# Where the operands of TensorE start in memory: a transformer kernel with longer tiles and shifted activations

## The chip, the core and the metric

The kernel runs on one core of a Trainium2 chip. The metric is the device time of one execution in microseconds (us), the median of several runs; lower is better.

## The reference, cut to what matters

Two blocks follow each other on 256 tokens of width 1024, in fp32. The first block runs two layers, the second one. Every layer is a projection of the normed input, a mixer (attention, a gated recurrence or a convolution), an output projection and a feed-forward network (FFN):

```python
for l in range(DEPTH):                       # 2 layers
    h = rmsnorm(x, norm_mix[l])
    proj = h @ w_in[l]
    ...
    merged = jax.nn.sigmoid(ga) * (y_attn @ w_proj_attn[l]) + jax.nn.sigmoid(gb) * (y_hgrn @ w_proj_hgrn[l])
    x = x + merged @ w_out[l]
    h = rmsnorm(x, norm_ffn[l])
    g, u = jnp.split(h @ w_ffn_in[l], 2, axis=-1)
    x = x + (jax.nn.silu(g) * u) @ w_ffn_out[l]
```

The second block does `[attn, u] @ w_o` and one more FFN, with its inputs scaled and shifted by a vector from `c @ ada_w`.

## The kernel before

All large products run on TensorE in the type fp32r, each as three matmuls: an operand is split into a high part H and a rest L, and H·H, H·L and L·H are summed (`mm3`, L781). ScalarE makes H with a copy, VectorE makes L with a subtraction (`split_into`, L887; `do_split`, L720, for the weights). In every matmul one operand is stationary (loaded by its own instruction, 128 columns) and the other is moving (streamed past it).

- **Moving activations, stationary weights.** In `pair_mm` (L786), `proj_mm` (L795) and `out_mm` (L896) the weights `wH`, `wL` are stationary, 128 columns at a time, and 256 tokens of an activation move: `xH`, `xL` (the normed input, `act_pair`, L873), `ya` and `yh` (the mixer's outputs, tiles `b4`, L1162 and L1289), `mH`, `mL` (the merged output, tiles `E`, L1314) and `H`, `L` of the FFN (tiles `t512`, L1382). The profile calls these moving tiles x, b, E and t.
- **Stationary activations, moving weights.** In `token_mm` (L804), `first_tm` (L1332) and `out_tm` (L908) the activations are stationary and 512 columns of weights move. `out_tm` is the second block's output projection and its FFN's.

In `out_mm` and `pair_mm` matmuls of the FFN interleave: the output product of one step of 256 hidden units runs beside the input product of the next (`ffn`, L1355). Nothing of this order is written by hand: the kernel records its operations (`Recorder`, L350), and a list scheduler with its own costs, due times and buffer counts (`issue`, L428) gives every engine its order. The costs of fp32r matmuls there follow from the number of columns alone.

Weights come through a ring of 4 raw tiles and 6 pairs `wH`, `wL` (`weights`, L734), all DMAs from SyncE's queue.

A tile has an address per partition. The tiles lie one after the other in the order of their first use, after a region of 16384 bytes that is kept for dynamic DMAs. All lengths are rounded up to 128 bytes (`new`, L644). A constant `GAP` (L755) of 256 bytes pads the constants, and `PLACE = 28` words puts `xH` and `xL` 112 bytes into tiles that are 128 words longer than they need be. The layout that comes out, as the start of the operand modulo 256 bytes:

| operand | base of its tile | start |
|---|---|---|
| weights raw, wH, wL | 0 | 0 |
| xH, xL | 0 | 112 |
| b4 (ya, yh) | 0 | 0 |
| E (mH, mL) | 128 | 128 |
| t512 (H, L of the FFNs) | 128 | 128 |

E and t512 lie at 128 because the tile `em` (L1010), a single line of 128 bytes, comes ahead of them. Within a tile, slices of an fp32r operand follow each other at multiples of 512 bytes. Every one of these starts is the same modulo 512 too.

Of the kernel before, what the change touches and what calls it, by code (L numbers as in the profile page):

```python
# [15 lines left out]
F32 = mybir.dt.float32  # L16
F32R = mybir.dt.float32r
# [10 lines left out]
FF, NJ = 2816, 11  # L28
LINE = 128

GAP = 64

PLACE = 28
OUT_SHAPE = [256, 1024]
EPS = 1e-6
NEG = -1e30
# [583 lines left out]
def program(tc, I, out, pw, cw, tap=None, stop=None):  # L620
    nc = tc.nc
# [10 lines left out]
    with es:  # L632
# [3 lines left out]
        act = es.enter_context(tc.tile_pool(name="act", bufs=1))  # L636
        tmp = es.enter_context(tc.tile_pool(name="tmp", bufs=2))
# [3 lines left out]
        def body():  # L641
            uid = [0]

            def new(pool, shape, dt=F32, tag=None, bufs=None):  # L644
                n = int(np.prod(shape[1:]))
                line = LINE if dt == U8 else LINE // 4
                if pool is not psum and pool is not dram and n % line:

                    v = new(pool, [shape[0], -(-n // line) * line], dt, tag, bufs)[:, :n]
                    return v if len(shape) == 2 else v.rearrange("p (a b) -> p a b", a=shape[1])  # L650
                uid[0] += 1
                b = Buf(pool, shape, dt, f"{tag or 'c'}_{uid[0]}", tag, bufs or 1, "PSUM" if pool is psum else "SBUF")
                return View(b, np.arange(n).reshape([1] + list(shape[1:])), shape[0], ())

            def bank(tag="mm"):
                return new(psum, [128, 512], F32, tag=tag, bufs=4)

            def acc_banks():

                acc = [bank("side") for _ in range(4)]  # L660
                for a in acc[1:]:
                    a.buf.group = acc[0].buf.group
                return acc

            def t512(dt=F32):
                return new(tmp, [128, 512], dt, tag="t512", bufs=9)

            def b4(dt=F32):
                return new(act, [128, 1024], dt, tag="b4", bufs=11)

            def small(n, bufs=8):
                return new(tmp, [128, 32], F32, tag="small", bufs=bufs)[:, :n]
# [1 line left out]
            def v2(ap):  # L674
                return ap.rearrange("p (a b) -> p a b", a=2)

            def bc(ap, n):
                return ap[:, None, :].to_broadcast([ap.shape[0], n, ap.shape[1]])
# [18 lines left out]
            def P(name):  # L697
                o, n = pw[name]
                return prm[:, o:o + n]
# [32 lines left out]
            at = [0]  # L732
# [21 lines left out]
            msk = new(const, [128, 5, 32], U8)  # L754
            new(const, [128, GAP]).real()  # L755

# [29 lines left out]
            def pair_mm(ps, X):  # L786

                xH, xL = X
                for b in range(2):
                    H, L = weights()  # L790
                    for k in range(8):
                        sl = slice(k * 128, k * 128 + 128)
                        mm3(ps[:, b * 256:b * 256 + 256], H[:, sl], L[:, sl], xH[:, k], xL[:, k], k == 0, k == 7)
# [76 lines left out]
                V.tensor_copy(rstd, ps)  # L870
                return v, r, rstd

            def act_pair():  # L873
                return tuple(new(act, [128, 2048 + 128], F32R, tag=t, bufs=1)[:, PLACE:PLACE + 2048].rearrange("p (a b) -> p a b", a=8)
                             for t in ("xH", "xL"))

            def scaled_split(g, acc=None):
# [9 lines left out]
            def split_into(H, L, src, scale=None):  # L887

                if scale is None:
                    A(H, src, AF.Copy)  # L890
                    tt(L, src, H.bitcast(F32), OP.subtract)
                else:
                    A(H, src, AF.Copy, scale=scale)
                    stt(L, src, scale, H.bitcast(F32), OP.mult, OP.subtract)

            def out_mm(acc, aH, aL, first, last):  # L896

                n_k = aH.shape[1]
                W = [weights() for _ in range(n_k)]
                for p in range(4):  # L900
                    for kk in range(n_k):
                        H, L = W[kk]
                        for b in range(2):
                            sl = slice((2 * p + b) * 128, (2 * p + b) * 128 + 128)
                            mm3(acc[p][:, b * 256:b * 256 + 256], H[:, sl], L[:, sl], aH[:, kk], aL[:, kk],
                                first and kk == 0, last and kk == n_k - 1, clear=b == 0)
# [99 lines left out]
            def layer(l, first, X):  # L1006
                R.bias = NORM_BIAS if first else 0.0
                ms, rt, rstd = norm_x()
                R.bias = 0.0
                em, rtok = new(act, [128, 2], F32, tag="em"), new(act, [128, 2], F32, tag="rtok")  # L1010
                ts(em, ms, EPS, None, OP.mult)
                V.tensor_copy(rtok, rt)
                tap(f"rstd{l}", rstd)
# [45 lines left out]
                for t in range(2):  # L1059
                    n = 128 * (t + 1)  # L1060
# [98 lines left out]
                    A(av[:, t], ps, AF.Copy, scale=rtok[:, t:t + 1])  # L1159
                tap(f"av{l}", av)  # L1160

                ya = [b4(F32R).rearrange("p (a b) -> p a b", a=4) for _ in range(2)]  # L1162
                for c in range(4):
                    y = bank("side")
                    for h in (2 * c, 2 * c + 1):
# [46 lines left out]
                for lev in range(8):  # L1212
# [3 lines left out]
                    elif lev < 7:  # L1216
# [9 lines left out]
                        n = 64 // m  # L1226
                        for j in range(8):
                            t, h = divmod(j, 4)
# [21 lines left out]
                    if lev < 6:  # L1250
                        n = 512 // m
# [34 lines left out]
                    stt(s, e, 1.0, z, OP.add, OP.mult)  # L1286
                    ts(s, s, P(f"hn{l}"), None, OP.mult)

                yh = [b4(F32R).rearrange("p (a b) -> p a b", a=4) for _ in range(2)]  # L1289
                for p in range(2):  # L1290
                    ps = bank("side")
                    for b in range(2):
# [5 lines left out]
                    w = lambda ap: ap[:, 2 * p:2 * p + 2].rearrange("p a b -> p (a b)")  # L1298
# [12 lines left out]
                    gate.append(gt[:, (p % 2) * 512:(p % 2) * 512 + 512])  # L1311


                mH, mL = (new(act, [128, 8, 256], F32R, tag="E", bufs=2) for _ in range(2))  # L1314
                for p in range(4):
                    ps = [bank(), bank()]
                    proj_mm(ps[1], yh)
# [1 line left out]
                    a, b = t512(), t512()  # L1319
# [3 lines left out]
                    w = lambda ap: ap[:, 2 * p:2 * p + 2].rearrange("p a b -> p (a b)")  # L1323
# [31 lines left out]
            def ffn(X, rstd, ada=None, out_mm=out_mm, first=None):  # L1355

                acc = acc_banks()
                pend = None
                for j in range(NJ + 1):
                    cur = None  # L1360
                    if j == 0 and first is not None:
                        pend = first
                        continue
                    if j < NJ:
                        pg = bank()
                        pair_mm(pg, X)
                        pu = bank()
                        pair_mm(pu, X)
                    if pend is not None:
                        out_mm(acc, pend[0], pend[1], j == 1, j == NJ)  # L1370
                    if j < NJ:
                        s, a = t512(), t512()
                        if rstd is not None:
                            z, u = t512(), t512()
                            tt(v2(z), v2(pg), bc(rstd, 2), OP.mult)
                            A(s, z, AF.Silu)
                            tt(v2(u), v2(pu), bc(rstd, 2), OP.mult)
                            tt(a, s, u, OP.mult)
                        else:
                            A(s, pg, AF.Silu)  # L1380
                            tt(a, s, pu, OP.mult)
                        H, L = t512(F32R), t512(F32R)  # L1382
                        split_into(H, L, a)
                        pend = (v2(H), v2(L))
                    if ada is not None:
                        ada(j)
                return acc
# [34 lines left out]
            def ada_steps(l):  # L1422
                cact = b4()
                DMA.dma_start(cact, I["c"].to_broadcast([128, 1024]))
                A(cact, cact, AF.Silu)

                def go(j):
                    for i in ([12 * l + j] if j < 12 else []):
                        w = new(act, [128, 2, 1024], F32, tag="E", bufs=2)
                        DMA.dma_start(w, I["ada"][i])  # L1430
                        for b in range(2):
                            V.scalar_tensor_tensor(w[:, b], w[:, b], 1.0, cact, op0=OP.mult, op1=OP.mult,
                                                   accum_out=MOD[:, 2 * i + b:2 * i + b + 1])
                return go
# [26 lines left out]
            for i, n in enumerate(("mix", "ffn")):  # L1461
                a = new(const, [128, 8])
                stt(a, mod[f"sc{i + 1}"], 1.0, P(f"{n}_pre_g"), OP.add, OP.mult)
                b = new(const, [128, 8])
# [87 lines left out]
            for tag, n in (("iq", 16), ("AT1", 16), ("cr", 8), ("sr", 8), ("qnc", 8), ("qns", 8), ("knc", 8), ("kns", 8)):  # L1552
                n = min(n, 16 * GROUPS - len(taps))
                if n > 0:
                    t = new(act, [128, n, 32], F32, tag=tag)
                    w = P("cw4")[:, len(taps):len(taps) + n]
                    tt(t, bc(C("ident32"), n), w[:, :, None].to_broadcast([128, n, 32]), OP.mult)
                    taps += [t[:, k] for k in range(n)]
            X = modulated("mix")
            xt = new(act, [128, 2048], F32, tag="E", bufs=2).rearrange("p (t n) -> p t n", t=2)  # L1560
            for t in range(2):
                for h in range(2):
                    ps = bank("side")
# [25 lines left out]
            R.bias = 0.0  # L1589
            tap("cum", cum)  # L1590

            ub = new(act, [128, 2048], F32, tag="E", bufs=2)[:, :1144].rearrange("p (c t) -> p c t", c=4)
            V.memset(ub[:, :, 0:30], 0.0)
            u4s = []
            ud = new(dram, [128, 4, 286])
# [37 lines left out]
            av = b4().rearrange("p (a b) -> p a b", a=2)  # L1633
            for t, ps in enumerate(token_mm(X)):
                A(av[:, t], ps, AF.Copy)
            mH, mL = act_pair()
            ts(C("low"), C("fut"), NEG, None, OP.mult)
            pens = (C("low")[:, 128:], C("low"))
            for c in range(4):
# [9 lines left out]
            for c in range(4):  # L1649
# [9 lines left out]
                for j in range(4 * GROUPS, 31):  # L1659
                    w = cwt[:, c * 31 + j:c * 31 + j + 1]  # L1660
# [53 lines left out]
```

## Time and profile before

| what | us |
|---|---|
| runs | 1131.61, 1129.08, 1130.52 |
| median | 1130.52 |
| the profiled execution, its own time | 1129.97 |
| its span, first to last instruction | 1128.2 |

Mean granted TensorE clock of the profiled execution: 0.992 of full speed. [...] "mm" and "side" are two sets of PSUM banks: `side<-t,wH` is a matmul into a side bank with t moving and wH stationary.

### The profile page before, as it was taken

To read this page: it belongs to the slowest core of one execution; us is meant where nothing else is said; L and a number is where in the kernel's file an instruction comes from. 1 tells how busy PE (TensorE), PEld (TensorE's weight loads), DVE (VectorE), ACT (ScalarE), POOL (GpSimd) and SP (SyncE) were. 2 spreads that over 40 slices of the span, in tenths; PEclk is the share of its full clock that TensorE was granted. 3 is DMA by queue.
4 is the path that set the end of the run, shared out by engine and by line. 5 is a ranking of instruction groups with operands and counts; after the bars stand their busy time and mean duration, and the time that the engine had idled before them with its cause. 6 is when DMAs were issued, how large, how long until landed. Compare 5 with 4: busy or idle time off the path is not lost.

```text
span 1128.2 us, 22970 instructions
## 1 busy us (share of the span) xinstructions
PE 1097.2 (97%) x9388; PEld 1034.5 (92%) x9388; DVE 857.5 (76%) x1590; ACT 595.5 (53%) x905; POOL 7.2 (1%) x16
## 2 busy tenths in 40 slices
PE   6999999999999999999999999999899989999996
PEld 6988999999999999888999999999798578999995
DVE  7999976899966589998676998756879668554554
ACT  6744694644444467446744544444754665443442
POOL 1000000000000000000000000000000000000000
PEclk9999999999999999999999999999999999999998
DMA  7553534689956543643345899655457225556550
GB/s 263 186 180 111 197 123 169 207 314 337 335 190 217 189 154 117 210 146 133 132 172 196 288 346 334 218 201 195 145 176 201 95 76 184 175 186 219 189 169 37
DMA packets 59992, 217.47 MB, mean 193 GB/s; under 512 B 6872, under 2 KB 10096, under 8 KB 56816
## 3 DMA queue, kind: packets, MB, share of 16 engines
q1 hardware_dynamic: 59888, 216.02, 55.8%
q8 instruction: 73, 1.20, 0.4%
q14 instruction: 31, 0.25, 0.1%
HBM read 214.19 MB, written 1.63 MB: 191 GB/s over the span
## 4 chain that ended last, share of the span: by engine, by line
PE 89%; DVE 6%; ACT 3%; issue 1%; DMA 1%; SPq 0%; DVEq 0%; ACTq 0%
PE mm L400 60%; PE side L400 29%; ACT t L400 2%; DVE t L400 1%; DVE b L400 1%; DVE wL L400 1%; DMA raw<-in_W 1%; DVE small L400 1%; ACT wH L400 1%; ACT L604 0%; DVE c L400 0%; DVE xL L400 0%; DVE AC L400 0%; SPq L400 0%; DVE sc L400 0%
## 5 line engine op out<-in xcount | busy, mean ns | idle before, releaser
L400 ACT ACTIVATE wH<-raw 128x1024 fp32r<-128x1024 f32 (+1 forms) x390 | 369.0, 968 | 400.5 <-PE mm L400 221.1
L400 DVE TENSOR_TENSOR wL<-raw,wH 128x1024 fp32r<-128x1024 f32 (+1 forms) x390 | 425.6, 1112 | 151.3 <-ACT wH L400 149.4
L400 PE MATMUL mm<-xH,wH 128*128 128x256 f32 x1760 | 486.8, 279 | 9.2 <-ACT wH L400 9.2
L400 PE MATMUL mm<-xH,wL 128*128 128x256 f32 x1760 | 488.3, 280 | 0.8 <-DVE wL L400 0.8
L400 PE MATMUL mm<-xL,wH 128*128 128x256 f32 x1760 | 488.5, 279 | 0.5 <-DVE xL L400 0.5
L400 PEld LDWEIGHTS mm<-xH,wH 128*128 128x128 f32 x1760 | 330.6, 189 | 11.7 <-ACT wH L400 9.2
L400 PEld LDWEIGHTS mm<-xL,wH 128*128 128x128 f32 x1760 | 331.2, 189 | 3.4 <-issue 0.9
L400 PEld LDWEIGHTS mm<-xH,wL 128*128 128x128 f32 x1760 | 330.8, 189 | 3.5 <-DVE wL L400 1.7
L400 PE MATMUL side<-t,wH 128*128 128x256 f32 x704 | 127.6, 281 | 0.0
L400 PEld LDWEIGHTS side<-t,wH 128*128 128x128 f32 x704 | 108.2, 188 | 0.0
L400 PE MATMUL side<-t,wL 128*128 128x256 f32 x352 | 98.8, 281 | 0.0
L400 ACT ACTIVATE t<-t 128x512 f32<-128x512 f32 (+2 forms) x80 | 48.9, 620 | 39.8 <-DVE t L400 37.0
L400 PEld LDWEIGHTS side<-t,wL 128*128 128x128 f32 x352 | 66.2, 188 | 0.0
L400 DVE SCALAR_TENSOR_TENSOR E<-E,b 128x1024 f32<-128x1024 f32 x48 | 57.9, 1221 | 4.1 <-DMA E<-in_ada 3.9
L400 PE MATMUL side<-wH,t 128*128 128x512 f32 x176 | 57.3, 394 | 0.0
L400 DVE TENSOR_TENSOR t<-t,t 128x512 f32<-128x512 f32 (+2 forms) x78 | 53.1, 681 | 3.7 <-ACT t L400 2.9
L400 PE MATMUL mm<-b,wH 128*128 128x256 f32 x256 | 46.6, 283 | 0.0
L400 PE MATMUL side<-E,wH 128*128 128x256 f32 x256 | 46.4, 281 | 0.0
L400 DVE TENSOR_TENSOR t<-mm,rstd 128x512 f32<-128x512 f32 (+1 forms) x50 | 33.7, 678 | 14.4 <-PE mm L400 14.1
L400 PE MATMUL mm<-wH,xH 128*128 128x512 f32 x96 | 38.7, 412 | 1.9 <-ACT xH L400 1.9
L400 PEld LDWEIGHTS mm<-b,wH 128*128 128x128 f32 x256 | 39.9, 191 | 0.0
L400 PEld LDWEIGHTS side<-E,wH 128*128 128x128 f32 x256 | 39.3, 188 | 0.0
(205 smaller groups left out, 1198.7 us busy)
## 6 DMA issues: line engine op xcount, KB each, us to landing
raw<-in_W SPq DMA_DIRECT2D x348, 512.0 KB, 4.3
E<-in_ada SPq DMA_DIRECT2D x24, 1024.0 KB, 7.0
b<-c SPq DMA_DIRECT2D x16, 128.0 KB, 4.6
c<-in_xT SPq DMA_DIRECT2D x4, 256.0 KB, 5.1
raw<-in_W SPq DMA_DIRECT2D x4, 256.0 KB, 4.9
b<-in_c SPq DMA_DIRECT2D x2, 512.0 KB
out_y<-E SPq DMA_DIRECT2D x4, 256.0 KB, 2.0
c<-E SPq DMA_DIRECT2D x4, 143.0 KB, 3.4
```

Of the source, the lines that this page charges most:

```text
L400: op.emit = lambda: getattr(real, method)(*[get(a) for a in args], **{k: get(a) for k, a in kw.items()})
```

## The change

Moving activations all start 112 bytes past a multiple of 256 bytes, stationary ones that have tiles of their own at a multiple. For that the tiles t512, b4, E get 64 words (256 bytes) more, xH and xL have 64 spare words instead of 128, `em` grows from one line of 128 bytes to two, and what lies behind it moves up by 128 bytes, so that E and t512 have their bases at 0 modulo 256. The region for dynamic DMAs shrinks from 16384 to 8192 bytes. The mixer's pair of the second block (`act_pair(0)`) and `H`, `L` of the last FFN (`out_tm`) start at 0. The pair xH, xL that is moving in one product and stationary in another stays at 112. No operation, shape or wait is added or removed, and nothing that the scheduler looks at is changed. Lengths after: t512 2304 bytes, b4 4352, E and xH and xL 8448; these are odd multiples of 256, so that modulo 512 every second tile of a kind starts 256 bytes further than the others; xL stands 8448 bytes behind xH.

```diff
-GAP = 64
-
-PLACE = 28
+GAP, GAP_E = 64, 32
+
+PLACE, ROOM = 28, 64
+
+SCRATCH = 8192
...
-            def t512(dt=F32):
-                return new(tmp, [128, 512], dt, tag="t512", bufs=9)
-
-            def b4(dt=F32):
-                return new(act, [128, 1024], dt, tag="b4", bufs=11)
+            def t512(dt=F32, at=0):
+                return new(tmp, [128, 512 + ROOM], dt, tag="t512", bufs=9)[:, at:at + 512]
+
+            def b4(dt=F32, at=0):
+                return new(act, [128, 1024 + ROOM], dt, tag="b4", bufs=11)[:, at:at + 1024]
+
+            def b8(dt=F32, at=0):
+                return new(act, [128, 2048 + ROOM], dt, tag="E", bufs=2)[:, at:at + 2048]
...
-            def act_pair():
-                return tuple(new(act, [128, 2048 + 128], F32R, tag=t, bufs=1)[:, PLACE:PLACE + 2048].rearrange("p (a b) -> p a b", a=8)
+            def act_pair(at=PLACE):
+                return tuple(new(act, [128, 2048 + ROOM], F32R, tag=t, bufs=1)[:, at:at + 2048].rearrange("p (a b) -> p a b", a=8)
                              for t in ("xH", "xL"))
...
-                em, rtok = new(act, [128, 2], F32, tag="em"), new(act, [128, 2], F32, tag="rtok")
+                em, rtok = new(act, [128, 2 + GAP_E], F32, tag="em")[:, :2], new(act, [128, 2], F32, tag="rtok")
...
-                ya = [b4(F32R).rearrange("p (a b) -> p a b", a=4) for _ in range(2)]
+                ya = [b4(F32R, PLACE).rearrange("p (a b) -> p a b", a=4) for _ in range(2)]
...
-                yh = [b4(F32R).rearrange("p (a b) -> p a b", a=4) for _ in range(2)]
+                yh = [b4(F32R, PLACE).rearrange("p (a b) -> p a b", a=4) for _ in range(2)]
...
-                mH, mL = (new(act, [128, 8, 256], F32R, tag="E", bufs=2) for _ in range(2))
+                mH, mL = (b8(F32R, PLACE).rearrange("p (a b) -> p a b", a=8) for _ in range(2))
...
-                        H, L = t512(F32R), t512(F32R)
+
+                        at = 0 if out_mm is out_tm else PLACE
+                        H, L = t512(F32R, at), t512(F32R, at)
...
-            mH, mL = act_pair()
+            mH, mL = act_pair(0)
...
-    nc = bacc.Bacc("TRN2", target_bir_lowering=False, num_devices=1)
+    nc = bacc.Bacc("TRN2", target_bir_lowering=False, num_devices=1, dynamic_dma_scratch_size=SCRATCH)
```

The four other uses of a tile E (two loads of `ada`, the transposed x and the convolution's input) only get the longer tile, at 0.

## Rows read from the trace of the kernel before

**Rows 1.** The page: span, busy time by engine, the chain that ended last.

```profile
span 1128.2 us, 22970 instructions
...
PE 1097.2 (97%) x9388; PEld 1034.5 (92%) x9388; DVE 857.5 (76%) x1590; ACT 595.5 (53%) x905; POOL 7.2 (1%) x16
...
PE 89%; DVE 6%; ACT 3%; issue 1%; DMA 1%; SPq 0%; DVEq 0%; ACTq 0%
```

**Rows 2.** Waits of PE, longest: us in total, times, longest us.

```profile
PE mm L400 <- ACT wH L400: 9.2, 1, 9.2
PE mm L400 <- ACT xH L400: 4.4, 2, 2.5
PE mm L400 <- DVE wL L400: 0.8, 2, 0.5
```

**Rows 3.** Busy time by stretch: us, PE, PEld, DVE, ACT, POOL, granted clock, DMA share, GB/s.

```profile
187.00:232.00 45.00, 44.77 (x379) 44.57 (x379) 31.58 (x50) 21.58 (x30) 0.52 (x1) 1.00 0.61 206
232.00:412.00 180.00, 179.72 (x1551) 179.37 (x1550) 138.58 (x173) 85.13 (x99) 0.00 (x0) 1.00 0.72 251
...
559.00:612.00 53.00, 53.00 (x450) 53.00 (x449) 38.59 (x45) 25.68 (x31) 0.00 (x0) 1.00 0.52 179
612.00:812.00 200.00, 197.47 (x1701) 196.58 (x1699) 155.31 (x222) 98.56 (x124) 0.00 (x0) 1.00 0.71 251
812.00:820.00 8.00, 6.56 (x41) 5.03 (x42) 6.28 (x12) 5.79 (x13) 0.00 (x0) 0.79 0.17 66
...
929.00:940.00 11.00, 8.71 (x33) 7.03 (x34) 10.53 (x32) 7.70 (x20) 0.00 (x0) 0.69 0.18 59
```

**Rows 4.** Timeline of PE, 560.65 to 566.20: x moving, 49 steps apart.

```profile
560.65 0.28 PE L400 MATMUL mm<-xL,wH 128*128 128x256 f32 x1
...
566.20 0.28 PE L400 MATMUL mm<-xH,wL 128*128 128x256 f32 x1
```

**Rows 5.** The same, 566.43 to 577.82: 96 matmuls with b moving.

```profile
566.43 0.40 PE L400 MATMUL mm<-b,wH 128*128 128x256 f32 x2
...
577.82 0.28 PE L400 MATMUL mm<-b,wL 128*128 128x256 f32 x1
```

**Rows 6.** The same, back to x: from 577.94 11 steps to 579.25, then 5 from 579.36.

```profile
577.94 0.28 PE L400 MATMUL mm<-xL,wH 128*128 128x256 f32 x1
...
579.25 0.28 PE L400 MATMUL mm<-xH,wH 128*128 128x256 f32 x1
579.36 0.28 PE L400 MATMUL mm<-xL,wH 128*128 128x256 f32 x1
...
579.93 0.40 PE L400 MATMUL mm<-b,wH 128*128 128x256 f32 x2
```

**Rows 7.** The chain in time: start us, us, what (t moves, x, E, weights).

```profile
381.66 3.32 PE side L400 x28
384.98 10.03 PE mm L400 x88
...
606.61 14.02 PE side L400 x118
...
1076.70 3.25 PE side L400 x14
```

**Rows 8.** Groups of matmuls on PE, forms apart: count, then busy us, mean ns.

```profile
L400 PE MATMUL mm<-xL,wH 128*128 128x256 f32 x1760 | 488.5, 279 | 0.5 <-DVE xL L400 0.5
...
L400 PE MATMUL side<-t,wH 128*128 128x256 f32 x704 | 127.6, 281 | 0.0
L400 PE MATMUL side<-t,wL 128*128 128x256 f32 x352 | 98.8, 281 | 0.0
L400 PE MATMUL side<-wH,t 128*128 128x512 f32 x176 | 57.3, 394 | 0.0
L400 PE MATMUL mm<-b,wH 128*128 128x256 f32 x256 | 46.6, 283 | 0.0
L400 PE MATMUL side<-E,wH 128*128 128x256 f32 x256 | 46.4, 281 | 0.0
...
L400 PE MATMUL mm<-b,wL 128*128 128x256 f32 x128 | 36.0, 283 | 0.0
L400 PE MATMUL side<-E,wL 128*128 128x256 f32 x128 | 36.0, 281 | 0.0
```

**Rows 9.** Timeline of PE: weights moving, x stationary, 512 columns, 7 steps apart.

```profile
864.27 0.39 PE L400 MATMUL mm<-wL,xH 128*128 128x512 f32 x1
...
865.90 0.39 PE L400 MATMUL mm<-wH,xL 128*128 128x512 f32 x1
```

**Rows 10.** Groups on DVE and ACT that write split activations of 512 columns.

```profile
L400 DVE TENSOR_TENSOR t<-t,t 128x512 fp32r<-128x512 f32 x32 | 22.0, 687 | 2.9 <-ACT t L400 2.9
...
L400 DVE TENSOR_TENSOR xL<-t,xH 128x512 fp32r<-128x512 f32 x8 | 5.3, 671 | 0.2 <-ACT xH L400 0.2
...
L400 ACT ACTIVATE t<-t 128x512 fp32r<-128x512 f32 x32 | 20.1, 628 | 27.4 <-DVE t L400 27.4
...
L400 ACT ACTIVATE xH<-t 128x512 fp32r<-128x512 f32 x8 | 5.0, 625 | 0.1
```

**Rows 11.** DMA queues: packets, MB, share of 16 engines.

```profile
q1 hardware_dynamic: 59888, 216.02, 55.8%
q8 instruction: 73, 1.20, 0.4%
q14 instruction: 31, 0.25, 0.1%
```

**Rows 12.** Timeline of PE after weights moving: 11 steps to 1081.08, 8 to 1081.98.

```profile
1079.56 0.40 PE L400 MATMUL side<-wH,t 128*128 128x512 f32 x1
1079.79 0.28 PE L400 MATMUL mm<-xH,wH 128*128 128x256 f32 x1
...
1081.08 0.28 PE L400 MATMUL mm<-xH,wL 128*128 128x256 f32 x1
...
1081.98 0.28 PE L400 MATMUL mm<-xL,wH 128*128 128x256 f32 x1
```

More of the change, by code (lines that the diff above doesn't have):

```diff
@@ L1428, in go @@
                     for i in ([12 * l + j] if j < 12 else []):
-                        w = new(act, [128, 2, 1024], F32, tag="E", bufs=2)
+                        w = b8().rearrange("p (a b) -> p a b", a=2)
                         DMA.dma_start(w, I["ada"][i])
@@ L1559, in body @@
             X = modulated("mix")
-            xt = new(act, [128, 2048], F32, tag="E", bufs=2).rearrange("p (t n) -> p t n", t=2)
+            xt = b8().rearrange("p (t n) -> p t n", t=2)
             for t in range(2):
@@ L1590, in body @@
             tap("cum", cum)
-            ub = new(act, [128, 2048], F32, tag="E", bufs=2)[:, :1144].rearrange("p (c t) -> p c t", c=4)
+            ub = b8()[:, :1144].rearrange("p (c t) -> p c t", c=4)
             V.memset(ub[:, :, 0:30], 0.0)
```

## Prediction

> **What bounds the kernel now.** I read the page first. TensorE (PE) is busy for 97% of the span, and 89% of the chain that ended last runs through it; VectorE and ScalarE hold 9% of that chain together [rows 1]. Then the waits: PE's longest one is 9.2 us at the start of the kernel, before the first weights are there, and all waits for a weight's rest add up to 0.8 us in the whole run [rows 2]. So weights are in time. Then the stretches in which the change acts: in 187 to 232 and 559 to 612 us (the projections of ya and yh and the product of mH, mL in either layer) and in 232 to 412 and 612 to 812 us (the two FFNs with moving activations), PE's busy time fills the stretch but for 0 to 2.5 us, with VectorE at 70 to 78% and the DMA engines at 52 to 72% [rows 3]. Whatever a matmul saves there, the span saves.
>
> A busy PE is not yet a PE at its peak, so the question is what one matmul costs, start to start. The durations in the groups (279 to 283 ns) can't tell, as matmuls overlap; the starts can. All of the following are matmuls of 256 moving columns with 128 stationary ones at full clock:
>
> - x moving, start at 112 modulo 256: 49 steps in 5.55 us, 113.3 ns each [rows 4].
> - b moving, start at 0: 96 in 577.94 - 566.43 = 11.51 us, 119.9 ns [rows 5, 6].
> - E moving, start at 128: 118 in 14.02 us, 118.8 ns; t moving, start at 128: 28 in 3.32 us, 118.6 ns (other runs of t between 118.2 and 118.8; taken 118.5) [rows 7].
> - x again, but just after b: 11 steps in 1.31 us, 119.1 ns; then, with nothing else changed, 5 in 0.57 us, 114 ns [rows 6].
>
> The product, the type, the weights' starts (0) and the clock are the same in all four. What differs by kind is where the moving operand starts, and x needs some 11 matmuls after an operand of another start until it has its own pace again.
>
> **The change part by part.**
>
> Moved starts. t, b and E get x's start of 112. I take x's 113.3 ns for them, as that is the one row with this start.
> - t: 704 + 352 = 1056 matmuls [rows 8], each 118.5 - 113.3 = 5.2 ns less: 5.5 us.
> - b: 256 + 128 = 384 of them [rows 8], each 119.9 - 113.3 = 6.6 ns less: 2.5 us.
> - E: 384 of them [rows 8], each 118.8 - 113.3 = 5.5 ns less: 2.1 us.
> - x after t, E or b: the timeline has 51 such returns (39, 9 and 3). One with its full 11 matmuls costs 1.31 - 11 x 0.1133 = 0.06 us [rows 6]; and a run of 88 x after t took 10.03 us where 88 x 0.1133 = 9.97, again 0.06 [rows 7]. Some are shorter; at 0.05 us each they are 2.5 us, and they should go, since with one start for all there is nothing to return from.
>
> Sum: 5.5 + 2.5 + 2.1 + 2.5 = 12.6 us.
>
> Stationary operands that move to 0. In `out_tm` of the last FFN t goes from 128 to 0 (176 + 88 = 264 matmuls [rows 8]), in the second block's output projection xH, xL go from 112 to 0 (96). They have 512 moving columns of weights, at 0 before and after. With t at 128 one costs 3.25 / 14 = 232 ns [rows 7], with x at 112 (865.90 - 864.27) / 7 = 233 ns [rows 9]: no difference to speak of. No row has both operands at 0. Bounds from the 256-column rows doubled: 2 x 113.3 = 226.6 and 2 x 119.9 = 239.8 ns, so for 360 matmuls -2.0 to +2.8 us. I take 0, as the two rows with 512 columns agree so closely.
>
> Everything else costs nothing, and I name the cover. VectorE and ScalarE write split activations at 112 and at 128 in equal time (671 and 687 ns; 625 and 628 ns [rows 10]), and with VectorE at 78% or less in these stretches [rows 3] some tens of ns on a hundred such instructions would stay hidden behind PE; without the cover they would be 1 or 2 us. [...]
>
> A faster PE frees weight tiles sooner and so asks for weights 12.6 / 1130 = 1% faster: with the DMA at 0.72 in the busiest of these stretches that leads to no wait. What is late next is still PE.
>
> Clock. [...] All work ahead of them is moved forward by some 10 us, and how much matmul work falls into them can differ; 1.7 us either way goes into the range.
>
> The profiled execution took 1129.97 us, 0.55 below the median of the runs. 1130.52 - 12.6 = 1117.9; I say 1118.
>
> **The rivals.**
>
> *A switch of operand disturbs, not a switch of start.* After the product of 512 columns, too, x needs 1.29 us for 11 matmuls, 117 ns each, and then 0.90 us for 8, 113 ns [rows 12]; so the disturbance could come with any change of operand, t after x included. Then t, b and E would gain only beyond their own first 12: 603, 284 and 283 of them by their run lengths in the timeline, 603 x 5.2 + 284 x 6.6 + 283 x 5.5 ns = 6.6 us, and the returns stay. Time: 1130.5 - 6.6 = 1124. Against it: x goes on at 113.3 ns over every change of weight tile and bank within rows 4, and the first t after a settled x is already at t's pace.
>
> *The start does not matter.* x might be fast because of what it multiplies with or where it writes, and t and E slow because they go to side banks. Time 1130.5. Against it: b goes to the same banks as x and multiplies with the same kind of weights, and it is the slowest [rows 5]; and x itself has both paces within one run [rows 6]. [...] The rows, 113.3 to 119.9 ns, differ by kind, so the measurement decides against it.
>
> *Slower: starts count modulo 512.* With odd multiples of 256 bytes as tile lengths, xL and every second b, t and E now start at 112 + 256 modulo 512. Before, all x were at 112, all t and E at 128 and all b at 0 modulo 512 too, so no row shows such a start. If it is a poor one, every third x matmul, those with xL (1760 [rows 8]), runs at 118.5, and as x needs 11 matmuls to settle, none of the x settles any more: about 3,900 settled ones x 5.2 ns = 20 us, with no gain for t, b and E. Time 1130 + 20 = 1150. The point from which it decides: the loss on xL alone is 1760 x 5.2 = 9.2 us, so it turns the sign as soon as xL drags a third of xH along. Against it: 0 and 128, which differ by half of 256, are within 1.4 ns of each other, so what counts seems to repeat at 128 already.
>
> **How the numbers follow.** Forecast 0.72 (1118, own range 1114 to 1121 by the clock and the two bounds of the stationary operands); switch disturbs 0.10 (1124); start does not matter 0.08 (1130.5); slower 0.10 (1150). The range has to take in 8 in 10: the forecast's cases and the 1124, so 1114 to 1125. A measurement of this kernel can tell 0.2%, 2.3 us, from no change: faster by more are the first two, 0.82; within it the third, 0.08; slower the fourth, 0.10.
>
> **What would show it.** After: runs of t, b and E in the chain at 113 to 114 ns a matmul; x at 113.3 right after them; the groups' mean for these tiles near 275 to 277 instead of 281 to 283 ns; PE's busy time down by some 12 us; runs with weights moving still at 232 ns; the same counts and waits. The first rival would show 118 ns at the start of every run of t, the second t and b unchanged, the third x at 118 all along. I am wrong if the span moves by under 6 us or if a new wait of PE for weights takes up what the matmuls give.

## The result, and the profile after

The changed kernel takes 1117.3 us (median of 6 runs, 1115.63 to 1119.12), the kernel before 1131.07 (6 runs). The ratio is 0.9882, with a 95% interval of 0.9868 to 0.9896: 13.8 us less by the medians, where 12.6 were forecast. The profiled execution took 1115.63 us, 14.3 less than the profiled one of before, with a span of 1113.9 us. The order of instructions is the same on every engine; the line numbers are 2 higher.

The page of the changed kernel, the lines that answer to [rows 1] and [rows 11]:

```profile
span 1113.9 us, 22970 instructions
...
PE 1083.2 (97%) x9388; PEld 1022.3 (92%) x9388; DVE 855.8 (77%) x1590; ACT 595.4 (53%) x905; POOL 7.2 (1%) x16
...
q1 hardware_dynamic: 59888, 216.02, 57.7%
...
PE 87%; DVE 8%; ACT 3%; issue 1%; DMA 1%; SPq 0%; DVEq 0%; ACTq 0%
```

PE's busy time fell by 14.0 us, nearly all of the 14.3; its share of the span is what it was, 97%. VectorE and ScalarE are busy for as long as before, within 2 us. The chain that ended last runs through VectorE for 8% of the span, where it was 6%. Next, the longest waits of PE in the changed kernel, to set beside [rows 2] (us in total, times, longest us):

```profile
PE mm L402 <- ACT wH L402: 9.2, 1, 9.2
PE mm L402 <- ACT xH L402: 4.4, 2, 2.5
...
PE mm L402 <- DVE wL L402: 0.8, 2, 0.5
```

No new wait for weights has appeared, though PE now asks for them earlier. Then the chain of the changed kernel in order of time (start us, us, what), to set beside [rows 4, 5, 7]:

```profile
552.53 26.89 PE mm L402 x237
...
597.90 7.15 PE side L402 x63
...
656.82 9.97 PE mm L402 x88
...
685.38 3.63 PE side L402 x32
...
1062.72 3.20 PE side L402 x14
```

The first row holds x and b, 26.89 / 237 = 113.5 ns a matmul. The second is E, 7.15 / 63 = 113.5, where it was 118.8. The fourth is t, 3.63 / 32 = 113.4, where it was 118.5. The third is x after t, 88 matmuls in 9.97 us: exactly 88 x 113.3, with no slow start; before, it took 10.03. The last is the product with weights moving and t stationary, 3.20 / 14 = 229 ns, where it was 232: that one was not forecast. The groups of PE say the same for the tiles that were moved (count, busy us, mean ns):

```profile
L402 PE MATMUL side<-t,wH 128*128 128x256 f32 x704 | 122.4, 275 | 0.0
L402 PE MATMUL side<-t,wL 128*128 128x256 f32 x352 | 96.8, 275 | 0.0
L402 PE MATMUL side<-wH,t 128*128 128x512 f32 x176 | 56.6, 391 | 0.0
L402 PE MATMUL side<-E,wH 128*128 128x256 f32 x256 | 44.4, 275 | 0.0
L402 PE MATMUL mm<-b,wH 128*128 128x256 f32 x256 | 44.2, 275 | 0.0
```

281 and 283 ns became 275 for t, E and b alike [rows 8].

In what follows "the pace" is the distance from a matmul's start to the next one's, from all starts in a trace, waits left out; "settled" means that at least 12 matmuls with the same pair of starts came before (3 where 512 columns move). Starts are in bytes modulo 256. "112 on 0" stands for a moving operand at 112 and a stationary one at 0.

### The profile page after: what moved, and what is told of

The parts are those of the page before. It is cut to its first block, busy times and chain, and to the rows that moved or that the text cites. A ratio compares the mean times of both kernels' runs of the same rounds, so it can differ in the third digit from the quotient of the medians.

```text
span 1113.9 us, 22970 instructions
## 1 busy us (share of the span) xinstructions
PE 1083.2 (97%) x9388; PEld 1022.3 (92%) x9388; DVE 855.8 (77%) x1590; ACT 595.4 (53%) x905; POOL 7.2 (1%) x16
## 4 chain that ended last, share of the span: by engine, by line
PE 87%; DVE 8%; ACT 3%; issue 1%; DMA 1%; SPq 0%; DVEq 0%; ACTq 0%
PE mm L402 60%; PE side L402 27%; DVE wL L402 2%; ACT t L402 1%; DVE t L402 1%; DVE b L402 1%; DVE small L402 1%; DMA raw<-in_W 1%; DVE c L402 1%; ACT wH L402 1%; DVE xL L402 0%; ACT L606 0%; DVE AC L402 0%; DVE E L402 0%; SPq L402 0%
## 5 line engine op out<-in xcount | busy, mean ns | idle before, releaser
L402 PE MATMUL side<-t,wH 128*128 128x256 f32 x704 | 122.4, 275 | 0.0
L402 PE MATMUL mm<-b,wH 128*128 128x256 f32 x256 | 44.2, 275 | 0.0
L402 PE MATMUL mm<-wH,xL 128*128 128x512 f32 x96 | 38.7, 405 | 0.0
```

The source lines that it names most:

```text
L402: op.emit = lambda: getattr(real, method)(*[get(a) for a in args], **{k: get(a) for k, a in kw.items()})
```

## The experiments

**Moved back, the layout kept.** b, E and the FFNs' t move from 0 again; lengths, bases and the smaller region stay.

```diff
-                ya = [b4(F32R, PLACE).rearrange("p (a b) -> p a b", a=4) for _ in range(2)]
+                ya = [b4(F32R, 0).rearrange("p (a b) -> p a b", a=4) for _ in range(2)]
...
-                        at = 0 if out_mm is out_tm else PLACE
+                        at = 0
```

(`yh` and `mH`, `mL` likewise.)

> The changed kernel, with b, E and the FFNs' t moving from 0 instead of 112 (modulo 256 bytes); longer tiles, x at 112 and stationary operands at 0 stay. Theory (the start of the moving operand sets the pace): t, b and E go from 113.3 to about 119.9 ns a matmul, as b had at 0 in the kernel before, which is 1824 x 6.6 ns = 12.0 us, and x is slow again after each of them, 2.5 us: some 14 us over the changed kernel, near 1131. Rival (the lengths, the bases or the smaller region did it): the time of the changed kernel, near 1117, and t, b, E at 113.

Measured: 1131.08 us, 1.0002 of the kernel before (0.9993 to 1.0011). The whole gain is gone, so the lengths, the bases and the region for dynamic DMAs are worth nothing that the times show. The equality is in part a balance: by the traces t and E at 0 (119.7 and 119.8 ns on the mean) cost 1.8 us more than at 128 before, and the stationary operands, still at 0, 1.5 us less. In its chain:

```profile
607.10 14.17 PE side L402 x118
...
631.96 12.41 PE mm L402 x109
```

E at 0 takes 14.17 / 118 = 120.1 ns, and x beside it, at 112, 113.9.

**Stationary operands back at 112.** The edit touches the three places that the change had put at 0 (`first_tm`'s H and L, too; so do the later edits of these starts).

```diff
-                        at = 0 if out_mm is out_tm else PLACE
+                        at = PLACE
...
-            mH, mL = act_pair(0)
+            mH, mL = act_pair()
```

> The changed kernel, with the stationary activations of the last block's output products at 112 again: t of the last FFN and the mixer's pair. Theory (a stationary start of 0 made those matmuls with weights moving faster, 234 to 227 ns): 264 x 5.3 + 96 x 6.2 ns = 2.0 us over the changed kernel, and 233 ns a matmul. Rival (the two traces differ there for another reason, such as the place of the bases): the matmuls stay at 227 to 229 ns and the time within 0.5 us.

Measured: 1119.74 us, ratio 0.9907 (0.9891 to 0.9924); 2.4 us over the changed kernel's 1117.3, and the matmuls with t stationary settle at 233 ns; at 0, in the changed kernel, they settle at 227.5. So the start of the stationary operand matters, and the prediction's 0 for it was wrong.

**Weights at 112, too.**

```diff
-                    H = new(wp, [128, 1024], F32R, tag="wH", bufs=N_SPLIT)
+                    H = new(wp, [128, 1024 + ROOM], F32R, tag="wH", bufs=N_SPLIT)[:, PLACE:PLACE + 1024]
```

(L likewise, here and in the later edits of the weights.)

> The changed kernel with the weights' tiles wH, wL also beginning at 112, moving or stationary. If only the moving operand's own start counts: x, t, b and E stay at 113.3 ns, and the matmuls with weights moving from 112 get faster than 227 ns. If the distance from stationary to moving operand counts: it is 0 now for x, t, b, E, so they are near 120 ns, about 7176 x 6.6 = 47 us over the changed kernel; the 360 matmuls of the last block with stationary activations at 0 have a distance of 112, the other 288 one of 0, and go to 227 ns.

Measured: 1145.94 us in one run. Neither case came out: x, t, b and E go at 118.2 ns, not 113.3 (so a moving start of 112 is not good by itself) and not 120 (so 112 on 112 is not the same as 0 on 0). With weights moving, 112 on 112 takes 230.7 ns and 112 on 0 takes 231. Its groups show the weights' share plainly, 284 ns where the changed kernel has 279:

```profile
L402 PE MATMUL mm<-xL,wH 128*128 128x256 f32 x1760 | 496.8, 284 | 0.5 <-DVE xL L402 0.5
```

**Other starts.** b at 48, E at 16, t at 240; stationary t at 144, the mixer's pair at 240.

```diff
-                ya = [b4(F32R, PLACE).rearrange("p (a b) -> p a b", a=4) for _ in range(2)]
+                ya = [b4(F32R, 12).rearrange("p (a b) -> p a b", a=4) for _ in range(2)]
...
-                        at = 0 if out_mm is out_tm else PLACE
+                        at = 36 if out_mm is out_tm else 60
...
-            mH, mL = act_pair(0)
+            mH, mL = act_pair(60)
```

> The changed kernel with other starts for each kind: moving b at 48, E at 16, t at 240, x as it was at 112; stationary t of the last FFN at 144, the mixer's pair at 240. If starts count modulo 128, t at 240 is as good as 112: 113.3 ns; if modulo 256, it is not. b at 48 would be as good if they count modulo 64. E at 16 tells whether any start off a multiple of 128 will do: then all are at 113.3 and the time is that of the changed kernel. If 112 alone is good: t 118 to 120, b and E too, some 13 us over the changed kernel. Stationary at 144, weights moving from 0, is a distance of 112 modulo 256: if the distance counts, 227 ns or less.

Measured: 1127.49 us in one run, 10 over the changed kernel. t at 240 takes 117.3 ns, b at 48 takes 118.3, E at 16 takes 117.3: starts do not count modulo 128 or 64, and "anything off a multiple of 128" will not do. Stationary at 144, which has a distance of 112 to weights moving from 0, takes 233 ns: with 512 columns that distance is not a good one.

**Two walks.** One kernel lets the weights walk in steps of 16 bytes past the moving operands at 112, the other lets the moving t walk past weights at 0, with b at 80, E at 176 and a walk of the last FFN's stationary t.

```diff
-                    H = new(wp, [128, 1024], F32R, tag="wH", bufs=N_SPLIT)
+                    o = 4 * (i // 6 % 16)
+                    H = new(wp, [128, 1024 + ROOM], F32R, tag="wH", bufs=N_SPLIT)[:, o:o + 1024]
```

```diff
-                        at = 0 if out_mm is out_tm else PLACE
+                        at = 4 * ((j + 11 * l) % 16) if out_mm is not out_tm else 4 * ((0, 1, 2, 4, 5, 6, 10, 11, 12, 13, 14)[j])
```

> The changed kernel with the start of the weights' tiles wH, wL walking in steps of 16 bytes, a new start every 6 tiles: 0, 16, ... 240, then 0 again; x, t, b, E move from 112. It maps the stationary start against a moving start of 112. Theory A (the pair of starts counts, and 112 against 0 is a narrow good point): settled stretches are at 113.3 ns for weights at 0 and between 116 and 120 at most other starts, so that the time is some 5000 to 6500 x 5 ns = 25 to 32 us over the changed kernel, 1142 to 1150. Theory B (anything off the bad points will do, and both at 112 was one of those): most of the 15 other starts are at 113.3 and the time within 10 us of the changed kernel.

> The changed kernel with the moving t of the two first FFNs walking in steps of 16 bytes from 0 to 240 by hidden step, b at 80 and E at 176; weights stay at 0; in the last FFN the stationary t walks over 16, 32, 64, 80, 96, 160, 176, 192, 208 and 224. Theory A (112 is a narrow good point): t at 113.3 ns at 112 alone, 117 to 120 elsewhere, b and E 117 to 119, some 10 us over the changed kernel, 1127. Theory B (a broad good region around 112, to the middle between 16 and 240 where 117 was measured): 80 to 176 are near 113.3, so b and E as well, and the time is 3 to 5 us over the changed kernel. For stationary t: 227 ns at 0 and 233 at 112, 128 and 144, 229 at 240; if it rises with the distance from 0, 16, 32 and 224 are under 230 and 64 to 176 over it.

Measured: 1144.61 and 1128.99 us, one run each; both fit the narrow point (theory A). In the chain of the second, the runs of t at 176, 192 and 208 in the second FFN:

```profile
646.55 3.11 PE side L402 x26
...
662.42 3.17 PE side L402 x28
...
678.49 3.57 PE side L402 x30
```

119.6, 113.2 and 119.0 ns: there is a second good start, and it is as narrow. Order them by distance (start of the moving operand less that of the stationary one, modulo 256), and the two walks agree within 0.8 ns at 12 of the 16 distances; at 0, 32, 128 and 224 they lie 1.3 to 2.5 ns apart. Settled paces in ns (in the walk of t: from the 9th matmul on, as its runs are short; b at 80, E at 176 and x at 112 are counted with t there). Weights at 112 past x at 112 (distance 0), here 117.5, took 118.2 over the whole run above.

| distance | t walks, weights 0 | weights walk, moving 112 |
|---|---|---|
| 0 | 120.0 | 117.5 |
| 16 | 118.7 | 118.0 |
| 32 | 116.8 | 118.5 |
| 48 | 118.3 | 118.3 |
| 64 | 117.8 | 118.3 |
| 80 | 119.7 | 119.9 |
| 96 | 119.9 | 120.0 |
| **112** | **113.7** | **113.7** |
| 128 | 118.7 | 120.0 |
| 144 | 118.5 | 117.7 |
| 160 | 117.3 | 117.2 |
| 176 | 119.2 | 119.3 |
| **192** | **113.3** | **113.4** |
| 208 | 119.4 | 119.2 |
| 224 | 118.3 | 119.8 |
| 240 | 116.8 | 117.2 |

With 512 columns of weights moving from 0, the stationary t takes 226.7 ns at 16, 227.4 at 0, 229.6 at 192, 229.9 at 176 and 231 to 234 at the others: another order, without a point as sharp.

**Two ways to a distance of 192.** The first puts all activations at 192 on weights at 0; the second leaves them at 112 and puts the weights, and the stationary operands of the last block's output products, at 176. All distances are the same in both. The changed kernel ran beside them.

```diff
-PLACE, ROOM = 28, 64
+PLACE, ROOM = 48, 64
```

```diff
-                    H = new(wp, [128, 1024], F32R, tag="wH", bufs=N_SPLIT)
+                    o = 44
+                    H = new(wp, [128, 1024 + ROOM], F32R, tag="wH", bufs=N_SPLIT)[:, o:o + 1024]
...
-                        at = 0 if out_mm is out_tm else PLACE
+                        at = 44 if out_mm is out_tm else PLACE
...
-            mH, mL = act_pair(0)
+            mH, mL = act_pair(44)
```

> The changed kernel with 192 bytes in place of 112 for x, t, b and E. Distance theory (what counts is the start of the moving less that of the stationary operand, modulo 256, and 112 and 192 are both good): 113.3 ns for all four as in the changed kernel; and the 288 matmuls in which x is stationary and weights move from 0 have a distance of 64 instead of 144, 229.6 instead of 233.1 ns: 1.0 us under the changed kernel, near 1116. Rival (192 was good for the few matmuls of t in the walk alone, by what stood around them): t, b, E, x at 117 to 120 and the time 10 to 35 us over it.

> The kernel of the run before with the same distances but other starts: weights at 176, moving x, t, b, E at 112 (distance 192), stationary operands of the last block's output products at 176 (distance 0), x stationary at 112 with weights moving from 176 (distance 64). Distance theory: the time of the run before, near 1116, and 113.3, 227 and 229.6 ns. Rival (the stationary start counts by itself, as both at 112 gave 117.5 where both at 0 gave 120.0): some of these paces differ; 231 ns in place of 227 for the 360 matmuls with distance 0 would be 1.3 us.

> The changed kernel once more, as it is, beside the runs of this call: 1117.3 as before, for the comparison with 192 and with the shifted starts.

Measured: 192 on 0 takes 1133.11 us (ratio 1.0011, 0.9997 to 1.0025), the shifted starts 1114.99 (0.9867, 0.9853 to 0.9882), the changed kernel 1117.42 (0.9882, 0.9869 to 0.9895). The last two intervals overlap a little; with the later runs of the shifted starts and the first ones of the changed kernel it is 8 runs with a median of 1115.0 against 10 with one of 1117.4. So the distance alone is not the rule, and my theory of it fell with the first of these. The chain of the kernel with 192 on 0 shows what happened, twice t and x in the first FFN, then t and x in the second:

```profile
383.79 3.30 PE side L402 x28
387.09 10.36 PE mm L402 x88
...
646.64 2.95 PE side L402 x26
649.58 9.75 PE mm L402 x86
```

In the first FFN a matmul takes 117.8 ns (10.36 / 88), in the second 113.4 (9.75 / 86): same code, same starts, same trace. In the stretches without other products one finds either 117.8 or 113.3 ns from the 13th matmul on, nearly nothing between, and the pace that a stretch comes to it keeps, for 1513 matmuls in the first FFN and 1500 in the second. Pair 192 on 0 has two settled paces, and which one a stretch gets is fixed within its first dozen matmuls. What picks it is not shown: the same small products stand ahead of the two FFNs, and yet they differ. The twelve runs lie between 1127.82 and 1136.29 us. With 112 on 176 the paces of the 6056 settled matmuls lie at 113 to 114 ns (10th and 90th percentile); its chain, t and x in the second FFN:

```profile
653.49 3.17 PE side L402 x28
656.66 9.97 PE mm L402 x88
```

Why it beats the changed kernel can be counted, for the first two terms by settled paces. Weights moving past x at 112 take 227.1 ns from 176 and 233.1 from 0 (288 matmuls, 1.7 us less); the 360 with both at 176 take 230.3 instead of 227.5 (1.0 us more); and x's mean over 5,074 matmuls of 256 columns is 113.70 instead of 114.05, as it settles sooner after other products (1.8 us less): after runs of t with 512 columns its first 12 matmuls take 113.3 to 114.1 ns, in the changed kernel 116.5 or 116.6. Together 2.5 us; measured 2.4.

**A finer walk.** t moves in steps of 4 bytes around 112 and 192, b from 196, E from 116.

```diff
-                        at = 0 if out_mm is out_tm else PLACE
+                        at = 0 if out_mm is out_tm else (22, 23, 24, 25, 26, 27, 28, 29, 30, 31, 33, 42, 43, 45, 46, 47, 48, 49, 50, 51, 53, 54)[j + 11 * l]
```

(b and E: 49 and 29 words.)

> The changed kernel with the moving t of the first two FFNs walking in steps of 4 bytes over 88 to 124 (112 in it), then 132, 168 to 172, 180 to 204, 212 and 216; b at 196, E at 116; weights at 0. If the good points are single starts of 4 bytes: only 112 and 192 at 113.3, all else 116 to 121, the time about 10 us over the changed kernel. If they are lines of 16 bytes: 112 to 124 and 192 to 204 alike at 113.3, b and E too, the time 2 to 4 us over it.

Measured: 1131.32 us in one run, 14 over the changed kernel. The good points are single starts of 4 bytes: 108 takes 120.0 ns, 112 takes 113.5, 116 takes 121.5; 188 takes 119.5, 192 takes 113.3, 196 takes 121.6. Starts that are not multiples of 16 are on the whole worse, up to 122, and b and E stand at such starts (121.7 and 121.5 ns on the mean); so the time came out 4 us over what was expected.

**Everything at 112 and 176.** With stationary activations at 112 as well, no exceptions for them are left in the code.

```diff
-                    H = new(wp, [128, 1024], F32R, tag="wH", bufs=N_SPLIT)
+                    o = 44
+                    H = new(wp, [128, 1024 + ROOM], F32R, tag="wH", bufs=N_SPLIT)[:, o:o + 1024]
...
-                        at = 0 if out_mm is out_tm else PLACE
+                        at = PLACE
...
-            mH, mL = act_pair(0)
+            mH, mL = act_pair()
```

> Every activation at 112, moving or stationary, and every weight at 176: the kernel of the run with all starts shifted, with the stationary operands of the last block's output products at 112 instead of 176. If the pair of starts sets the pace, as weights moving from 176 past x at 112 took 227.5 ns there, those 360 matmuls go from 230.3 to 227.5 ns: 1.0 us less, near 1114 (ratio 0.986 to the kernel before), and the best of all. Rival (227.5 came from what stands around x's products, not from the pair): they stay at 230 and the time at 1115.

> The kernel with all starts shifted once more, as it is (weights 176, moving activations 112, the last block's stationary operands 176), beside the run before: 1115, ratio 0.9867. As the pace after each entry was the good one everywhere in its first trace, the runs should agree within 0.3%; if weights at 176 had two settled paces as 192 against 0 had, single runs would lie 5 to 20 us higher.

Measured: 1114.58 us (ratio 0.9855, 0.9839 to 0.9872), and beside it the shifted starts again 1115.21 (0.9861, 0.9846 to 0.9876). The two intervals overlap, so the 0.6 us between them is not shown by the times; by the traces the 360 matmuls did go from 230.3 to 227.1 ns. In the chains, first of this kernel, then of the one with stationary operands back at 112 and weights at 0, 34 matmuls with t stationary at 112 take 7.73 and 7.98 us, 227 and 235 ns each:

```profile
1094.67 7.73 PE side L402 x34
```

```profile
1098.72 7.98 PE side L402 x34
```

Both kernels beat the one before by 1.4% and the changed one by 2 to 3 us. A second settled pace has not shown for weights at 176: the four runs of this kernel agree within 0.1%, the eight with the shifted starts lie between 1113.86 and 1117.68 us.

## Why the prediction was right, and where it was not

The time, 1117.3 us, lies 0.7 us under the forecast. That closeness is in part luck: 1.2 us more were saved than forecast, and the median of the kernel before rose by 0.55 with three more runs. By its own steps, from all starts in the two traces (waits left out):

| step | forecast us | measured us |
|---|---|---|
| t, 1056 | 5.5 | 5.3 (118.4 to 113.4 ns) |
| b, 384 | 2.5 | 2.5 (119.8 to 113.3) |
| E, 384 | 2.1 | 2.1 (118.7 to 113.3) |
| x after t, b, E | 2.5 | 2.5 (mean of x 114.56 to 114.06, 5,076 of them) |
| stationary operands to 0, 360 | 0 | 1.5 (t 232.4 to 228.6; the mixer's pair 233.3 to 227.6) |
| sum | 12.6 | 13.9 |

The profiled executions differ by 14.3; 0.4 us are not assigned. The own range's upper end was added up wrongly: 1117.9 + 2.8 + 1.7 is 1122, not 1121; the stated range, to 1125, covers both.

- *The mechanism.* Right, and shown by undoing it: with the layout kept and the starts back at 0, the gain is gone (1131.08 us). The pace of the one row with this start, 113.3 ns [rows 4], carried over to t, b and E (113.3 to 113.4).
- *The returns of x.* Right: x has no slow start after t, b and E any more. In sum its matmuls there stood 2.63 us above 113.3 ns each before, and stand 0.15 above it now. It keeps a slow start after products of 512 columns, which have other starts: 116.5 or 116.6 ns over its first 12 matmuls after those with t.
- *Switch of operand disturbs (0.10).* Refuted by the same rows: t runs at 113.4 ns from its first matmul.
- *The start does not matter (0.08).* Refuted: with the moving start held at 112, the start of the weights alone moves the pace between 113.4 and 120.0 ns. Why the weights' start acts on the pace was not tried.
- *Starts count modulo 512 (0.10).* Refuted: in the changed kernel xH at 112 and xL at 368 modulo 512 have 114.0 and 114.1 ns, the two halves of t, b and E agree within 0.4. My argument against this rival, that 0 and 128 being alike meant a repeat at 128, was poor all the same: 240 is not 112 (117.3 ns). Its point of decision was wrong as well: under this rival every second b, t and E is poor too, which leaves them a gain of 5.0 us, and the 9.2 us lost on xL alone turn the sign, without any of xH.
- *Stationary operands to 0.* This is the term that failed: taken as 0 because 112 and 128 cost the same [rows 7, 9], with bounds of -2.0 to +2.8 us. It brought 1.5 us, inside the bounds. Two equal starts said nothing of a third; the rows of b and t, which do differ by start, were the better hint.
- *Clock.* The two stretches below full clock [rows 3] are still there, granted 0.66 in 795 to 805 us and 0.69 in 914 to 925. The lower level in them is a granted 0.50: in the kernel before it holds for 3.4 us (0.50 in every half microsecond from 813.5 to 816.5) and 6.8 us (929.5 to 936), in the changed kernel for 6.8 us both times (797 to 803.5 and 916.5 to 923). The 1.7 us either way that the range has for the clock were an estimate, and no run shows them; what the traces show is 3.4 us more at 0.50 in the first stretch, by an estimate from the granted clock at most 1.7 us against the change. So up to 1.7 us more than the 0.4 may be unassigned.
- *The smaller region.* Its 0 was an estimate, and no run changes it alone. In the run with the layout kept and the starts back at 0, the longer tiles, the bases and the region together show no cost: 1131.08 us, 1.0002 of the kernel before (0.9993 to 1.0011).

What stays open is why 112 and 192 are good. The runs show that the pair of starts sets the pace, mostly by their distance, with good points no wider than the 4 bytes of the finest walk, and that a pair can have two settled paces. What inside the chip makes them was not tried, and all runs have one type, one kernel and one core.

## What to carry to other kernels

Where fp32r matmuls with 256 moving columns follow each other without a gap, read their distance from start to start, kind by kind: kinds that differ only in where their tiles lie (here x with 113.3 ns and b with 119.9) are worth a look at addresses. Let the starts walk within one run, moving and stationary ones both, and read the settled paces from the trace; then run the best pair in full, several times, as a pair that looked as good for a few dozen matmuls can settle at another pace for whole stages (192 on 0: 113.2 ns over 28 matmuls in the walk, 117.8 in the whole first FFN). A tile of other length ahead of them moves all starts behind it, so pad it.

## What had not been expected of the hardware

- A start of 4 bytes more or less is worth 6 to 8 ns of 113 (112 against 108 and 116), 6 to 7%.
- The pace depends on the stationary operand's start as much as on the moving one's: 113.4 ns for x at 112 on weights at 0 or 176, 117 to 120 at the 14 other multiples of 16.
- One pair, 192 on 0, keeps either 113.3 or 117.8 ns for 1500 matmuls in a row, and nothing here shows what picks it; 112 on 0 and 112 on 176 came to between 113.3 and 113.7 in every trace.
- With weights moving, 512 columns take 226.7 to 234 ns by the pair of starts, and the good pairs are others: 0 on 0 or 16, and 176 on 112.
